# The first norm by token, and a new order of the first pairs, in a hybrid decoder trunk

## The chip, the cores and the metric

The kernel runs on 1 core of one Trainium2 chip, as one program that is launched once. The metric is device time in microseconds (us), the median of several executions. Engines are called by the profile's names: PE is TensorE (matrix products), PEld its loading of weights, DVE is VectorE, ACT is ScalarE, POOL is GpSimd, SP is SyncE, which issues nearly all DMAs here.

## The reference

One layer (`DEPTH` = 1) of a decoder trunk with 1024 features, for 1024 prompt tokens (one sequence) and 32 sample tokens (eight sequences of four) that share the weights. Cut to what matters here:

```python
mod = jax.nn.silu(c) @ w_ada[l] + b_ada[l]
sh1, sc1, gt1, sh2, sc2, gt2 = [m[:, None, :] for m in jnp.split(mod, 6, axis=-1)]
h = _rmsnorm(x, g_pre_mix[l]) * (1.0 + sc1) + sh1
z = h @ w_in[l]
...                      # gated mixing, a gated recurrence and a convolution on parts of z
y = jnp.concatenate([ya, yb, yc], axis=-1) @ w_out[l]
x = x + gt1 * _rmsnorm(y, g_post_mix[l])
h = _rmsnorm(x, g_pre_mlp[l]) * (1.0 + sc2) + sh2
y = jnp.square(jax.nn.relu(h @ w_up[l])) @ w_down[l]
x = x + gt2 * _rmsnorm(y, g_post_mlp[l])
```

`_rmsnorm` divides each token by the root of its mean square over the 1024 features. The change is in the third and fourth lines alone: the first norm, its shift and scale, and the first products with `w_in`.

## The kernel before, in words

Features lie on partitions (eight blocks k of 128), tokens along the free axis. The 1056 tokens are three chunks c of `CW` = 352; chunk 2 holds the sample tokens, whose shift and scale differ by sequence, so it is handled apart and first (`FIRST` = 2, 0, 1). Every product is made of three fast products: each operand is split into a high part (`hi`, a cast) and the rest (`lo`), and hi*hi + lo*hi + hi*lo is summed. A weight split is a cast on ACT (`whi`) and a subtraction on DVE (`wlo`).

The queues of the engines are in program order: the instructions of an engine run as the code issues them. `PE`, `ACT`, `DVE`, `POOL` and `SP` are wrappers that also keep a planner's clock by a price for each instruction; nearly all instructions therefore carry line L113 in the profile, and DMAs L107. The products of the first two weight blocks (`first_product`, L744) are issued past the wrapper. Later tasks (convolution, recurrence, norms, later shifts and gates) are generators that a planner starts at due times; none of them runs before the first products are done.

The stage in question, before:

- SP loads, in order: small vectors, x of chunks 2, 0, 1 (three parts each: `KK` = blocks 0-2, 3-5, 6-7), the identity, `ada_load(0)` (four loads of 512 KB: the weights of shift and scale for blocks 0 and 1), rows 0-1 of the first two weight blocks, `ada_load(2)`, rows 2-3. `ada_load(4)`, rows 4-7 and `ada_load(6)` follow later. `ada_load(4)` reuses the buffers of 0, and `ada_load(6)` those of 2.
- `first_squares`: ACT squares x, PE multiplies the squares with a matrix of ones and so sums them over features, with the sum of a token on every partition (`stps`, 352 columns). For chunk 1 DVE adds two blocks ahead of it. `first_rstd`: ACT takes the square root, DVE the reciprocal, of 128 x 352 values.
- `warm`: matmuls of zeros that keep PE at work.
- `ada_first(b)`: 32 matmuls for shift and scale of blocks b and b+1 (`adaps`); `ada_copy` copies the result from PSUM on ACT; `ada_turn` turns it on PE (`adapt`) and makes `mod` and `G1` on DVE.
- `first_h(p)` makes h of blocks 2p and 2p+1 for all chunks: `plain(0)`, `last()` (chunk 2), `plain(1)`, `last_lo()`, on DVE and ACT in turns. `scale_x` multiplies chunk 2 by its 1/rms on DVE ahead of that. `split_first` splits rows of the first two weight blocks, `split_next` a whole later block.
- `both(c, k)` is six products: block k, chunk c, both weight blocks.
- `first_blocks` goes over the four pairs p of blocks. In a pair: `both(0, k)`, the turn of the next pair, its h, then the weight split; `both(2, k)`, `both(1, k)`; the `ada_first` of the pair after the next; then `both` of block k+1 for chunks 0, 2, 1. `first_evacs` makes block 7 and takes the results out.

Buffers that matter: five PSUM banks in `pb`, three in `pm`; six buffers of 128 x 8 x 352 in `hp`, which hold the squares (`sqs`, three) and the h (six), so three of the h take over buffers of squares.

Of the kernel before, what the change touches and what calls it, by code (L numbers as in the profile page):

```python
# [7 lines left out]
F32 = mybir.dt.float32  # L8
F32R = mybir.dt.float32r
I32 = mybir.dt.int32  # L10
AF = mybir.ActivationFunctionType
ALU = mybir.AluOpType
# [3 lines left out]
CW = 352  # L16
# [143 lines left out]
def trunk_kernel(ctx: ExitStack, tc: tile.TileContext, xT, cT, wada0, wada, vec, cst, msk, win, wout, wup,  # L160
# [143 lines left out]
    def fetch():  # L304
        if jobs:
            src, shape = jobs.pop(0)
            raw = wp.tile(shape, F32, tag="raw", name="raw", bufs=3)
            if isinstance(src, list):
                for i, x in enumerate(src):
                    SP.dma_start(out=raw[:, 2 * i:2 * i + 2], in_=x)  # L310
            else:
                SP.dma_start(out=raw, in_=src)
            raws.append((raw, shape))
# [74 lines left out]
    def ada_load(b):  # L388

        at = []  # L390
        for k in range(0, 8, 2):
            t = ada_at[b % 4 * 2 + k // 2]
            SP.dma_start(out=t, in_=wada0[b // 2, :, k:k + 2, :])
            at += [t[:, 0, :], t[:, 1, :]]
        return b, at

    def ada_first(raws):

        b, at = raws
        ps = pb.tile([128, 128], F32, tag="b", name="adaps")  # L400
        for k in range(8):
            for g in range(4):
                PE.matmul(out=ps[32 * g:32 * g + 32, :], lhsT=scT[:, k, :], rhs=at[k][:, g * 128:g * 128 + 128],
                          start=(k == 0), stop=(k == 7), skip_group_check=True)
            if k % 2:
                yield b, ps

    def ada_copy(first):
        b, ps = first
        sb = mp.tile([128, 128], F32, tag="adasb", name="adasb")  # L410
        ACT.copy(out=sb, in_=ps)
        return b, sb

    def ada_turn(copied):

        b, sb = copied
        pt = pb.tile([128, 2, 2, 32], F32, tag="b", name="adapt")
        PE.transpose(out=pt.rearrange("p v i n -> p (v i n)"), in_=sb, identity=ident)
        add_bada(pt[:, :, :, 0:9], b, 2, 2, 8)
        DVE.scalar_tensor_tensor(out=G1[:, b:b + 2, :], in0=mod[:, 8 + b:10 + b, :],  # L420
                                 scalar=1.0, in1=bc9(V_GPM)[:, b:b + 2, :], op0=ALU.add, op1=ALU.mult)
# [187 lines left out]
    def load3(src, name):  # L609
        ts = []  # L610
        for kk, (k0, n) in enumerate(KK):
            t = e3(f"{name}{kk}")
            SP.dma_start(out=t[:, 0:n, :], in_=src[:, k0:k0 + n, :])
            ts.append(t)
        return lambda kk: ts[kk][:, 0:KK[kk][1], :]
# [26 lines left out]
    def load_rows(rows):  # L642
        for src, raw in raw_first:
            SP.dma_start(out=raw[:, rows, :], in_=src[:, rows, :])

    def split_first(rows):
        for (_, raw), (hi, lo) in zip(raw_first, w_first):
            ACT.copy(out=r(hi[:, rows, :]), in_=raw[:, rows, :])
            DVE.tensor_tensor(out=r(lo[:, rows, :]), in0=raw[:, rows, :], in1=hi[:, rows, :], op=ALU.subtract)

    xs_in = {c: load3(xT[c], f"x{c}_") for c in FIRST}
    SP.dma_start(out=ident, in_=cst[:, K_ID:K_ID + 128])
    ada_raws = [ada_load(0)]
    load_rows(slice(0, 2))
    ada_raws.append(ada_load(2))
    load_rows(slice(2, 4))

# [5 lines left out]
    def warm(n):  # L663

        for i in range(n):
            PE.matmul(out=wps[:, 0:128], lhsT=zero[:, 0:128], rhs=zero[:, 0:128], start=True, stop=True)

    sums = {}

    def first_squares(c, kk, added):  # L670

        k0, n = KK[kk]
        sq = sqs[c]
        if kk == 0:
            sums[c] = pb.tile([128, CW], F32, tag="b", name="stps")
        ACT.activation(out=sq[:, k0:k0 + n, :], in_=xs_in[c](kk), func=AF.Square)
        if added:
            DVE.tensor_tensor(out=sq[:, k0, :], in0=sq[:, k0, :], in1=sq[:, k0 + 1, :], op=ALU.add)
        for k in range(k0, k0 + n):
            if not added or k != k0 + 1:  # L680
                PE.matmul(out=sums[c], lhsT=ones, rhs=sq[:, k, :], start=k == 0, stop=k == (6 if added else 7))

    def first_rstd(c):
        ACT.activation(out=rstds[c], in_=sums.pop(c), func=AF.Sqrt, scale=1.0 / 1024, bias=eps)
        DVE.reciprocal(out=rstds[c], in_=rstds[c])

    def spans(p):

# [5 lines left out]
    def scale_x(c, p):  # L694
        for kk, a, b, k in spans(p):
            t = xs_in[c](kk)[:, a:b, :]
            DVE.tensor_tensor(out=t, in0=t, in1=rep(rstds[c], b - a), op=ALU.mult)

    def first_h(p):


        if p == 0:
            h.update({c: (hc(f"h{c}hi"), hc(f"h{c}lo")) for c in range(NCH)})

        def plain(c):
            ts = [(xs_in[c](kk)[:, a + i, :], k + i) for kk, a, b, k in spans(p) for i in range(b - a)]
            for t, k in ts:
                DVE.scalar_tensor_tensor(out=t, in0=t, scalar=G1[:, k, 0:1], in1=rstds[c], op0=ALU.mult,
                                         op1=ALU.mult)
                ACT.activation(out=r(h[c][0][:, k, :]), in_=t, func=AF.Identity, bias=sh1[:, k, 0:1], scale=1.0)  # L710
            for t, k in ts:
                DVE.scalar_tensor_tensor(out=r(h[c][1][:, k, :]), in0=t, scalar=sh1[:, k, 0:1],
                                         in1=h[c][0][:, k, :], op0=ALU.add, op1=ALU.subtract)

        def last():
            w = CW - NS
            for kk, a, b, k in spans(p):
                n = b - a
                u = xs_in[2](kk)[:, a:b, :]
                us_ = u[:, :, w:]  # L720
                DVE.tensor_tensor(out=b4(us_), in0=b4(us_), in1=seqs(G1[:, k:k + n, :]), op=ALU.mult)
                DVE.tensor_tensor(out=b4(us_), in0=b4(us_), in1=seqs(sh1[:, k:k + n, :]), op=ALU.add)
                for i in range(n):
                    ACT.activation(out=u[:, i, 0:w], in_=u[:, i, 0:w], func=AF.Identity, scale=G1[:, k + i, 0:1],
                                   bias=sh1[:, k + i, 0:1])
                ACT.copy(out=r(h[2][0][:, k:k + n, :]), in_=u)

        def last_lo():
            for kk, a, b, k in spans(p):
                hi, lo = (t[:, k:k + b - a, :] for t in h[2])  # L730
                DVE.tensor_tensor(out=r(lo), in0=xs_in[2](kk)[:, a:b, :], in1=hi, op=ALU.subtract)

        plain(0)
        last()
        plain(1)
        last_lo()

    pss = {}

# [7 lines left out]
    def both(c, k):  # L747
        for m, i in ((0, 0), (0, 1), (1, 0), (1, 1), (0, 2), (1, 2)):
            first_product(c, k, m, i)

    warm(14)
    for i, c in enumerate(FIRST):
        for kk in range(3):
            first_squares(c, kk, i == 2)
            if i == 1 and kk == 0:
                first_rstd(2)
                scale_x(2, 0)
        if i == 0:
            nc.scalar.preload_act_table(AF.Sqrt)
    first_rstd(0)  # L760
    parts = ada_first(ada_raws.pop(0))
    for i in range(3):
        next(parts)
        warm(2)
    first_rstd(1)
    nc.scalar.preload_act_table(AF.Sigmoid)
    split_first(slice(0, 2))
    copied = ada_copy(next(parts))
    ada_raws.append(ada_load(4))
    load_rows(slice(4, 8))  # L770
    warm(2)
    ada_turn(copied)
    first_h(0)
    scale_x(2, 1)
    for at in ada_first(ada_raws.pop(0)):
        warm(2)
    copied = [ada_copy(at)]
    ada_raws.append(ada_load(6))
    fetch()
    SP.dma_start(out=cst_t[:, K_BLK:K_BLK + 256], in_=cst[:, K_BLK:K_BLK + 256])  # L780

    def first_blocks():


        for p in range(4):
            k = 2 * p
            both(0, k)
            if p < 3:
                ada_turn(copied.pop())
                first_h(p + 1)  # L790
                if p < 2:
                    scale_x(2, p + 2)
                    split_first(slice(2 * p + 2, (4, 8)[p]))
                else:
                    split_next()
            else:
                ACT.copy(out=r(means), in_=cst_t[:, K_BLK:K_BLK + 256])
            both(2, k)
            both(1, k)
            if p < 2:  # L800
                for at in ada_first(ada_raws.pop(0)):
                    pass
                copied.append(ada_copy(at))
            if p < 3:
                for c in (0, 2, 1):
                    both(c, k + 1)

    def first_evacs(evacs):
        credit.update(dve=0.0, act=0.0, pe=0.0)
# [1286 lines left out]
```

## Time and profile before

| | us |
|---|---|
| median of 3 runs | 1260.38 |
| the three runs | 1264.3, 1258.51, 1260.38 |
| the profiled execution | 1263.86 |
| its span in the profile | 1262.1 |
| granted clock of PE, mean | 0.99 |

| engine | busy, us | share of the span |
|---|---|---|
| PE | 1221.9 | 97% |
| PEld | 1171.4 | 93% |
| DVE | 902.0 | 71% |
| ACT | 533.6 | 42% |
| POOL | 63.0 | 5% |

How to read the views: a row of the timeline has start, length, engine, line, operation, output<-inputs, shapes and count, and in brackets how long the engine was idle before it and what ended that. A row of the busy time by stretches has the stretch, its length, the busy time of PE, PEld, DVE, ACT and POOL with the number of instructions, the granted clock, the share of the DMA engines' time and GB/s. All times are from the start of the span. The ends of matmuls are modelled, so the distance from start to start tells more than a length. A float32 matmul shows as two passes.

### The profile page before, as it was taken

To read this page: it belongs to the slowest core of one execution; us is meant where nothing else is said; L and a number is where in the kernel's file an instruction comes from. 1 tells how busy PE (TensorE), PEld (TensorE's weight loads), DVE (VectorE), ACT (ScalarE), POOL (GpSimd) and SP (SyncE) were. 2 spreads that over 40 slices of the span, in tenths; PEclk is the share of its full clock that TensorE was granted. 3 is DMA by queue.
4 is the path that set the end of the run, shared out by engine and by line. 5 is a ranking of instruction groups with operands and counts; after the bars stand their busy time and mean duration, and the time that the engine had idled before them with its cause. 6 is when DMAs were issued, how large, how long until landed. Compare 5 with 4: busy or idle time off the path is not lost.

```text
span 1262.1 us, 20853 instructions
## 1 busy us (share of the span) xinstructions
PE 1221.9 (97%) x8614; PEld 1171.4 (93%) x8614; DVE 902.0 (71%) x1469; ACT 533.6 (42%) x989; POOL 63.0 (5%) x107
## 2 busy tenths in 40 slices
PE   9999999999899999999999999999999999999995
PEld 7888889999889999899999999999999999999994
DVE  5799889688658768866686657657666765765766
ACT  6513464684854746555423312322331331231533
POOL 1000020211010011000000000000000000000001
PEclk9999999999999999999999999999999999999998
DMA  9458401111111466243201211210211120111218
GB/s 367 170 217 277 168 26 52 43 59 47 35 43 40 151 192 182 85 134 106 79 18 50 68 34 34 68 49 19 68 50 34 51 68 32 36 67 35 108 18 210
DMA packets 48846, 113.22 MB, mean 90 GB/s; under 512 B 10336, under 2 KB 24832, under 8 KB 48624
## 3 DMA queue, kind: packets, MB, share of 16 engines
q1 hardware_dynamic: 44432, 99.22, 22.9%
q0 software_dynamic: 4320, 12.68, 4.3%
q8 instruction: 67, 1.10, 0.4%
q14 instruction: 27, 0.22, 0.1%
HBM read 101.75 MB, written 10.14 MB: 89 GB/s over the span
## 4 chain that ended last, share of the span: by engine, by line
PE 78%; DVE 11%; ACT 6%; DMA 3%; issue 2%; POOL 0%; SPq 0%; DVEq 0%; ACTq 0%
PE pmt L113 71%; DVE acc L113 2%; PE adaps L113 1%; DMA rawada<-in_wada 1%; DVE T L113 1%; PE pmt L744 1%; DVE wlo L113 1%; DMA o<-in_xT 1%; ACT K L113 1%; ACT vf L113 1%; DVE q L113 1%; PE sc L113 1%; DVE rsq L113 1%; ACT relu L113 1%; PE ob L113 1%
## 5 line engine op out<-in xcount | busy, mean ns | idle before, releaser
L113 PE MATMUL pmt<-ah,whi 128*128 128x352 f32 (+2 forms) x744 | 244.0, 328 | 7.9 <-DVE acc L113 5.8
L113 PE MATMUL pmt<-al,whi 128*128 128x352 f32 (+2 forms) x744 | 241.3, 324 | 1.3 <-DVE al L113 1.3
L113 PE MATMUL pmt<-ah,wlo 128*128 128x352 f32 (+2 forms) x744 | 240.1, 323 | 0.0
L113 DVE TENSOR_TENSOR acc<-acc,pmt 128x352 f32<-128x352 f32 (+1 forms) x320 | 158.5, 510 | 91.8 <-PE pmt L113 91.6
L113 DVE TENSOR_TENSOR wlo<-raw,whi 128x1024 fp32r<-128x1024 f32 (+2 forms) x113 | 134.5, 1192 | 46.2 <-ACT whi L113 46.2
L113 ACT CAST whi<-raw 128x1024 fp32r<-128x1024 f32 (+2 forms) x113 | 114.2, 1014 | 107.9 <-PE pmt L113 105.8
L113 PEld LDWEIGHTS pmt<-ah,whi 128*128 128x128 f32 x744 | 139.7, 188 | 15.3 <-DVE acc L113 10.7
L113 PEld LDWEIGHTS pmt<-al,whi 128*128 128x128 f32 x744 | 139.9, 188 | 4.2 <-DVE al L113 2.0
L113 PEld LDWEIGHTS pmt<-ah,wlo 128*128 128x128 f32 x744 | 139.9, 188 | 0.4
L113 ACT COPY acc<-pmt 128x352 f32<-128x352 f32 x63 | 28.4, 452 | 196.7 <-PE pmt L113 161.8
L113 PE MATMUL pmt<-h22hi,wlo 128*128 128x352 f32 x256 | 82.7, 323 | 0.0
L113 PE MATMUL pmt<-h22hi,whi 128*128 128x352 f32 x256 | 82.5, 322 | 0.0
L113 PE MATMUL pmt<-h22lo,whi 128*128 128x352 f32 x256 | 82.3, 322 | 0.0
L113 DVE SCALAR_TENSOR_TENSOR cva<-cvx,vec_t,cva 128x1024 f32<-128x1024 f32 x60 | 77.7, 1295 | 1.2
L113 PE MATMUL pmt<-s,whi 128*128 128x352 f32 x312 | 75.6, 324 | 0.0
L113 ACT ACTIVATE relu<-pmt 128x352 f32<-128x352 f32 x57 | 26.4, 463 | 104.2 <-PE pmt L113 101.3
L113 DVE TENSOR_TENSOR al<-rsq,ah 128x352 fp32r<-128x352 f32 x96 | 49.1, 523 | 15.7 <-ACT ah L113 9.6
L113 PE MATMUL pmt<-h1hi,whi 128*128 128x352 f32 x168 | 55.7, 332 | 2.6 <-DVE gq L113 2.6
L113 PE MATMUL pmt<-h2hi,whi 128*128 128x352 f32 x168 | 56.7, 337 | 0.0
L113 PE MATMUL pmt<-h0hi,whi 128*128 128x352 f32 x168 | 55.5, 330 | 0.8 <-DVE gq L113 0.8
L113 PEld LDWEIGHTS pmt<-s,whi 128*128 128x128 f32 x312 | 54.5, 188 | 0.0
L113 DVE TENSOR_TENSOR rsq<-relu 128x352 f32<-128x352 f32 x45 | 23.5, 523 | 43.0 <-ACT relu L113 41.8
(391 smaller groups left out, 2941.0 us busy)
## 6 DMA issues: line engine op xcount, KB each, us to landing
rawada<-in_wada SPq DMA_DIRECT2D x48, 512.0 KB, 8.3
raw<-in_wup SPq DMA_DIRECT2D x36, 512.0 KB, 3.5
raw<-in_wdn SPq DMA_DIRECT2D x48, 256.0 KB, 3.1
raw<-in_win SPq DMA_DIRECT2D x22, 512.0 KB, 3.6
raw<-in_wout SPq DMA_DIRECT2D x20, 512.0 KB, 3.5
raw<-in_wdn SPq DMA_DIRECT2D x12, 512.0 KB, 3.5
x<-in_xT SPq DMA_DIRECT2D x6, 528.0 KB, 7.0
o<-in_xT POOLq DMA_DIRECT2D x6, 528.0 KB, 7.8
```

The lines of the kernel that those rows point to most:

```text
L113: return f(**kw)
L744: nc.tensor.matmul(out=pss[m, c], lhsT=r(w_first[m][i % 2][:, k, :]), rhs=r(h[c][i // 2][:, k, :]), start=k == i == 0, stop=k == 7 and i == 2)
```

## The change

Four parts:

1. The sums of the first norm are made by token. For each block, four matmuls take 88 tokens of the squares each as weights and one column of ones, and add into a tile of 88 x 4 sums, which a matmul with zeros has cleared first. ACT takes the square root of 88 x 4 values (`token_rms`, which exists for the last norm), DVE the reciprocal; `first_diagonal` multiplies it into four copies of the 88 x 88 identity, in a part of the squares' buffer; `by_feature` (exists too) spreads it over all partitions with a matmul with the ones, and ACT copies the result to `rstds`. The additions on DVE for chunk 1 go.
2. The identity is loaded ahead of x. x of chunk 1 is loaded behind the first shift and scale and the first weight rows, and it is squared and summed behind the first turn, between the first products. The Sqrt table is loaded before all squares, the Sigmoid table behind the last square root.
3. `first_h` returns its parts, so that the first pair can be issued in the order `plain(0)`, split, `both(0, 0)`, `last`, `last_lo`, `both(2, 0)`, `plain(1)`, with the squares of chunk 1 in between.
4. In the pairs, `both(0, k)` and `both(2, k)` come first, then `ada_first` of the next pair, `both(1, k)`, the turn, the weight split, and only then the next pair's h. `ada_first(2)`, `ada_load(6)`, the next weight load and the load of the constants move into the first pair.

```diff
-    xs_in = {c: load3(xT[c], f"x{c}_") for c in FIRST}
     SP.dma_start(out=ident, in_=cst[:, K_ID:K_ID + 128])
+    xs_in = {c: load3(xT[c], f"x{c}_") for c in FIRST[0:2]}
     ada_raws = [ada_load(0)]
     load_rows(slice(0, 2))
+    xs_in[1] = load3(xT[1], "x1_")
     ada_raws.append(ada_load(2))
     load_rows(slice(2, 4))
...
-    def first_squares(c, kk, added):
+    def first_squares(c, kk):
         k0, n = KK[kk]
         sq = sqs[c]
         if kk == 0:
-            sums[c] = pb.tile([128, CW], F32, tag="b", name="stps")
+            sums[c] = pb.tile([CW // 4, 4], F32, tag="b", name="sums")
+            PE.matmul(out=sums[c], lhsT=zero[:, 0:CW // 4], rhs=zero[:, 0:4], start=True, stop=False,
+                      skip_group_check=True)
         ACT.activation(out=sq[:, k0:k0 + n, :], in_=xs_in[c](kk), func=AF.Square)
-        if added:
-            DVE.tensor_tensor(out=sq[:, k0, :], in0=sq[:, k0, :], in1=sq[:, k0 + 1, :], op=ALU.add)
+        t = CW // 4
         for k in range(k0, k0 + n):
-            if not added or k != k0 + 1:
-                PE.matmul(out=sums[c], lhsT=ones, rhs=sq[:, k, :], start=k == 0, stop=k == (6 if added else 7))
-
-    def first_rstd(c):
-        ACT.activation(out=rstds[c], in_=sums.pop(c), func=AF.Sqrt, scale=1.0 / 1024, bias=eps)
-        DVE.reciprocal(out=rstds[c], in_=rstds[c])
+            for g in range(4):
+                PE.matmul(out=sums[c][:, g:g + 1], lhsT=sq[:, k, g * t:(g + 1) * t], rhs=ones[:, 0:1],
+                          start=False, stop=k == 7, skip_group_check=True)
+
+    def first_rms(c):
+        rts[c] = token_rms(sums.pop(c))
+
+    def first_diagonal(c):
+        t = CW // 4
+        rt = rts.pop(c)
+        DVE.reciprocal(out=rt, in_=rt)
+        d = sqs[c][0:t, 0, :]
+        DVE.tensor_tensor(out=d.rearrange("p (g t) -> p g t", t=t), in0=rep(ident[0:t, 0:t], 4),
+                          in1=rt.rearrange("p (g o) -> p g o", o=1).to_broadcast([t, 4, t]), op=ALU.mult)
+        return d
+
+    def first_rstd(c, d):
+        ACT.copy(out=rstds[c], in_=by_feature(d))
...
+    nc.scalar.preload_act_table(AF.Sqrt)
     warm(14)
-    for i, c in enumerate(FIRST):
-        for kk in range(3):
-            first_squares(c, kk, i == 2)
-            if i == 1 and kk == 0:
-                first_rstd(2)
-                scale_x(2, 0)
-        if i == 0:
-            nc.scalar.preload_act_table(AF.Sqrt)
-    first_rstd(0)
+    for kk in range(3):
+        first_squares(2, kk)
+    first_squares(0, 0)
+    first_rms(2)
+    d = first_diagonal(2)
+    first_squares(0, 1)
+    first_rstd(2, d)
+    first_squares(0, 2)
+    scale_x(2, 0)
+    first_rms(0)
+    d = first_diagonal(0)
+    warm(2)
+    first_rstd(0, d)
     parts = ada_first(ada_raws.pop(0))
     for i in range(3):
         next(parts)
         warm(2)
-    first_rstd(1)
-    nc.scalar.preload_act_table(AF.Sigmoid)
-    split_first(slice(0, 2))
-    copied = ada_copy(next(parts))
+    copied = [ada_copy(next(parts))]
     ada_raws.append(ada_load(4))
     load_rows(slice(4, 8))
     warm(2)
-    ada_turn(copied)
-    first_h(0)
-    scale_x(2, 1)
-    for at in ada_first(ada_raws.pop(0)):
-        warm(2)
-    copied = [ada_copy(at)]
-    ada_raws.append(ada_load(6))
-    fetch()
-    SP.dma_start(out=cst_t[:, K_BLK:K_BLK + 256], in_=cst[:, K_BLK:K_BLK + 256])
...
     def first_blocks():
+        ada_turn(copied.pop())
+        first_squares(1, 0)
+        plain, last, last_lo = first_h(0)
+        plain(0)
+        split_first(slice(0, 2))
+        both(0, 0)
+        first_squares(1, 1)
+        last()
+        first_squares(1, 2)
+        first_rms(1)
+        nc.scalar.preload_act_table(AF.Sigmoid)
+        last_lo()
+        d = first_diagonal(1)
+        both(2, 0)
+        first_rstd(1, d)
+        plain(1)
+        scale_x(2, 1)
         for p in range(4):
             k = 2 * p
-            both(0, k)
+            if p:
+                both(0, k)
+                both(2, k)
+            if p < 3:
+                for at in ada_first(ada_raws.pop(0)):
+                    if p == 0:
+                        warm(2)
+                copied.append(ada_copy(at))
+                if p == 0:
+                    ada_raws.append(ada_load(6))
+                    fetch()
+                    SP.dma_start(out=cst_t[:, K_BLK:K_BLK + 256], in_=cst[:, K_BLK:K_BLK + 256])
+            both(1, k)
             if p < 3:
                 ada_turn(copied.pop())
-                first_h(p + 1)
                 if p < 2:
-                    scale_x(2, p + 2)
                     split_first(slice(2 * p + 2, (4, 8)[p]))
                 else:
                     split_next()
+                plain, last, last_lo = first_h(p + 1)
+                plain(0)
+                last()
+                plain(1)
+                last_lo()
+                if p < 2:
+                    scale_x(2, p + 2)
+                for c in (0, 2, 1):
+                    both(c, k + 1)
             else:
                 ACT.copy(out=r(means), in_=cst_t[:, K_BLK:K_BLK + 256])
-            both(2, k)
-            both(1, k)
-            if p < 2:
-                for at in ada_first(ada_raws.pop(0)):
-                    pass
-                copied.append(ada_copy(at))
-            if p < 3:
-                for c in (0, 2, 1):
-                    both(c, k + 1)
```

More of the change, by code (lines that the diff above doesn't have):

```diff
@@ L666, in warm @@
             PE.matmul(out=wps[:, 0:128], lhsT=zero[:, 0:128], rhs=zero[:, 0:128], start=True, stop=True)
-    sums = {}
-    def first_squares(c, kk, added):
+    sums, rts = {}, {}
+    def first_squares(c, kk):
         k0, n = KK[kk]
@@ L731, in last_lo @@
                 DVE.tensor_tensor(out=r(lo), in0=xs_in[2](kk)[:, a:b, :], in1=hi, op=ALU.subtract)
[L733 to L736, printed above, removed]
+        return plain, last, last_lo
     pss = {}
```

## The prediction

> **What bounds the kernel now.** I read the busy time by stretches, the timeline of the first 63 us engine by engine, what TensorE (PE) waited for there, and the chain of waits. The change touches only what runs before the product of the third weight block, which begins at 62.95, so the question is how far that moment moves.
>
> ```profile
> 62.97:200.00 137.03, 136.41 (x1104) 120.83 (x1104) 125.82 (x150) 51.67 (x95) 10.79 (x20) 1.00 0.49 167
> 7.44:29.87 22.43, 22.43 (x203) 14.98 (x204) 13.85 (x20) 15.81 (x23) 0.00 (x0) 1.00 1.03 405
> 29.87:62.95 33.08, 30.68 (x278) 28.06 (x277) 25.59 (x56) 17.93 (x36) 0.25 (x2) 0.95 0.52 181
> 62.95 0.33 PE L113 MATMUL pmt<-h0hi,whome 128*128 128x352 f32 x1
> ```
>
> The first three lines give length, then busy time of PE, weight load, DVE, ACT, POOL, then granted clock, DMA share and GB/s. Behind the stage PE is busy 136.4 of 137.0 us and DVE 125.8, so neither has slack to swallow a delay: a us lost or won before 62.95 is a us of the end. From 7.44 to 29.87 PE has no gap at all: its own order of work sets the start of the products, although the DMA engines are full too (share 1.03). From 29.87 on it has 2.4 us of gaps and a clock of 0.95.
>
> ```profile
> 7.44 12.84 PE L113 MATMUL stps<-sq,cst_t 128*128 128x352 f32 x42
> 20.21 0.64 PE L113 MATMUL adaps<-rawada,scT 128*32 128x128 f32 x16
> 24.98 0.27 PE L113 MATMUL adapt<-cst_t,adasb 128*128 128x128 f32 x1
> 29.87 0.41 PE L744 MATMUL pmt<-h0hi,whi 128*128 128x352 f32 x1
> 30.92 0.27 PE L113 MATMUL adapt<-cst_t,adasb 128*128 128x128 f32 x1
> 33.29 1.96 PE L113 MATMUL adaps<-rawada,scT 128*32 128x128 f32 x64
> 36.23 0.32 PE L744 MATMUL pmt<-h2hi,whi 128*128 128x352 f32 x1
> 37.18 0.32 PE L744 MATMUL pmt<-h1hi,whi 128*128 128x352 f32 x1
> 40.94 0.43 PE L744 MATMUL pmt<-h0hi,wlo 128*128 128x352 f32 x1 [1.92 <-DVE wlo L113]
> 42.32 0.41 PE L113 MATMUL adapt<-cst_t,adasb 128*128 128x128 f32 x1
> 51.88 0.27 PE L113 MATMUL adapt<-cst_t,adasb 128*128 128x128 f32 x1
> 18.25 7.48 DMA rawada<-in_wada
> ```
>
> These are the timeline's PE rows (start, length, operation, count, wait) and one step of the chain of waits, which releases the first h. 21 matmuls with the ones (two passes each, 42) take 12.84 us, 0.61 each. The first shift/scale block takes 24.98 - 20.21 = 4.8 us with its warm matmuls, a later one 1.96. Six products of one block and chunk ("a sextet") take 37.18 - 36.23 = 0.95. The turns (adapt) stand at 24.98, 30.92, 42.32, 51.88: each releases mod and G and so the next h, and each follows the first sextet of its pair. The row at 40.94 is the stall that the weight splits cause by standing behind h on DVE.
>
> **The price of a sum by token.** The same sums by token are in the trace near its end:
>
> ```profile
> L113 PEld LDWEIGHTS sums<-cst_t,tots x16: 133/156/178, 1236.6 to 1247.9; 128*112 128x112 f32 x8, 128*64 128x64 f32 x8
> 1236.59 0.88 PEld L113 LDWEIGHTS sums<-cst_t,tots 128*112 128x112 f32 x8
> 1247.52 0.54 PEld L113 LDWEIGHTS sums<-cst_t,tots 128*64 128x64 f32 x8 [1.71 <-DVE tots L113]
> 1238.09 0.24 ACT L113 ACTIVATE rt<-sums,cst_t 112x4 f32<-112x4 f32 x1
> 1238.36 0.18 DVE L113 RECIPROCAL rt<-rt 112x4 f32<-112x4 f32 x1 [0.70 <-ACT rt L113]
> L113 DVE TENSOR_TENSOR diag<-cst_t,rt x2: 417/522/628, 1238.6 to 1248.7; 112x448 f32<-112x448 f32 x1, 64x256 f32<-64x256 f32 x1
> L113 ACT COPY acc<-pmt 128x352 f32<-128x352 f32 x63 | 28.4, 452 | 196.7 <-PE pmt L113 161.8
> ```
>
> Eight passes of 112 tokens step by (0.88 - 0.18)/7 = 0.100 us, of 64 tokens by (0.54 - 0.13)/7 = 0.058. The change has 88 tokens: halfway, 0.079. A feature block is four matmuls of two passes, 0.63 us against 0.61 before, and a chunk 5.05. So PE gains nothing by the new form; the third chunk, where DVE adds halved part of the matmuls (5 instead of 8, 3.1 us), loses 2.0. Each chunk also gets a zero matmul (two passes with 88 columns as weights, 0.16) and the spreading matmul (like one with the ones, 0.6). PE's work in the stage grows by 2 x 0.2 + 2.0 + 3 x 0.76 = 4.7 us, and two warm matmuls that stand in a wait. The unknown end: at 0.058 a chunk costs 3.7, at 0.100 6.4; three chunks give -4.0 to +4.0 us on PE, and since some of it fills stalls I keep about -3 to +3. The gain, on engines that do not set the end there:
>
> ```profile
> 13.10 2.35 DVE L113 RECIPROCAL rstd<-rstd 128x352 f32<-128x352 f32 x1 [7.79 <-ACT rstd L113]
> 16.30 1.60 DVE L113 TENSOR_TENSOR sq<-sq 128x352 f32<-128x352 f32 x3
> 10.58 1.08 ACT L113 ACTIVATE sq<-x 128x1056 f32<-128x1056 f32 x1
> 9.29 1.28 ACT L759 ACT_TABLE_LOAD   x1
> ```
>
> Three reciprocals (2.35 each) become 0.18 + about 0.52 for the diagonal, and the three additions go; DVE had 8.6 us idle in 7.44 to 29.87. The Sqrt table load moves ahead of the first x and is hidden there. The Sigmoid load moves behind the third square root, where its follower waits for PE's spreading matmul anyway.
>
> **Order on the queues.** Taking x's third chunk (1.4 MB at 405 GB/s, 3.5 us) out of the way lets the first shift/scale land 3.5 us sooner, about 17.1 instead of 12.0 + 8.6 = 20.6 (row below: the last of four is issued at about 12.0). The identity goes ahead of x and costs the first square 0.2. The third chunk now comes behind all of x, four loads of 512 KB and the first weight rows, some 7 MB: 17.3 us at 405 GB/s after a start near 3, an estimate of 21; it is first squared at 26.2, so the move costs nothing.
>
> ```profile
> 8.37 3.93 SPq L107 DMA_DIRECT2D rawada<-in_wada  x4
> rawada<-in_wada SPq DMA_DIRECT2D x16, 512.0 KB, 8.6
> ```
>
> The last shift/scale load waits for buffers of the second, which PE now frees only between about 36.8 and 41; behind it on SP's queue stand a weight load and the small constants. They land by 41 + 8.6 = 50, and are wanted at 61 and later. POOL issues nothing else. So no DMA ends on the path, by a cover of ten us.
>
> **The new lead-in, step by step (us).** First square ends 7.5; PE sums chunk 2 to 12.6 and blocks 0 to 5 of chunk 0 to 16.5, then spreads chunk 2's 1/rms (0.6). On ACT the copy of that result (0.45) stands ahead of the last square of chunk 0 (0.78), so PE waits from 17.1 to 18.55 (1.4). Blocks 6 and 7 to 19.8, two warm matmuls; square root, reciprocal and diagonal (0.24 + 0.2 + 0.52 with hand-overs) end at 21.1: a wait of 0.85. Spread to 21.7, shift/scale 4.6 us, first turn at 26.3, against 24.98: 1.3 later in spite of the earlier data. Now PE sums chunk 1 in between: it waits for the square that ACT starts only after the copy for the turn (0.76), 3 blocks, the first sextet (0.4 wait for the weight split), 5 blocks (0.55 wait), a sextet, the diagonal (0.35 wait), spread: 36.2. The second shift/scale with warm matmuls 4.8, a sextet, second turn at 42.0. Before it stood at 30.92. Of those 11 us, 1.9 are two sextets that used to come after it.
>
> **The cycle of the other pairs.** Before, a turn needed only the first sextet of its pair, and its shift/scale was done a pair earlier. Now turn p+1 stands behind both sextets 0 and 2, then shift/scale p+1, then sextet 1; and the second part of h2 is the last thing that DVE makes. So the work no longer overlaps:
>
> ```profile
> 42.78 0.20 DVE L113 TENSOR_TENSOR mod<-adapt,vec_t 128x36 f32<-128x36 f32 x1 [1.55 <-PE adapt L113]
> 48.35 0.89 DVE L113 TENSOR_TENSOR h2lo<-x,h2hi 128x704 fp32r<-128x704 f32 x1
> 40.47 0.76 DVE L113 TENSOR_TENSOR wlo<-raw,whi 128x256 fp32r<-128x256 f32 x2
> 49.95 1.29 DVE L113 TENSOR_TENSOR wlo<-raw,whi 128x512 fp32r<-128x512 f32 x2
> 58.57 1.22 DVE L113 TENSOR_TENSOR whome<-raw,whome 128x1024 fp32r<-128x1024 f32 x1
> ```
>
> Turn to mod 0.46, mod to the end of h2lo 49.24 - 42.78 = 6.46, and the weight split's DVE part, now ahead of h: 0.76, 1.29 and 1.22 (its casts on ACT run while PE still does the third sextet). From h2lo to the next turn PE needs 0.3 + 1.96 + 0.95 = 3.2. Cycles: 0.46 + 6.46 + 0.76 + 3.2 = 10.9, then 11.4. Turns at 42.0, 52.9, 64.3. The last h2lo at 64.3 + 8.1 = 72.4; then 0.3 + 0.95 + 18 products of 0.16 = 4.1. The stage ends at 76.5 instead of 62.95: +13.5. It counts what the change saves: the stalls for the split (1.92 and smaller) and the slow clock behind them are inside 62.95.
>
> **The clock.** In each cycle PE does four sextets (3.8 us) while it waits 6.5 to 8 us for h: about 3.3 us idle inside 4.2.
>
> ```profile
> 37.89:41.30 3.41, 1.19 (x6) 0.62 (x5) 3.33 (x7) 1.12 (x4) 0.12 (x1) 1.00 0.45 171
> 41.30:44.71 3.41, 3.41 (x14) 3.34 (x13) 1.70 (x5) 0.87 (x2) 0.00 (x0) 0.50 0.02 5
> 328.02:331.43 3.41, 1.75 (x11) 1.75 (x12) 3.41 (x7) 3.33 (x8) 0.00 (x0) 1.00 0.00 0
> 331.43:334.84 3.41, 2.95 (x48) 2.62 (x48) 3.31 (x5) 3.32 (x8) 0.00 (x0) 1.00 0.36 113
> 525.99:529.40 3.41, 1.50 (x9) 1.47 (x10) 2.57 (x4) 1.62 (x4) 0.00 (x0) 1.00 0.15 60
> 529.40:532.82 3.42, 3.42 (x14) 3.42 (x13) 3.35 (x7) 0.97 (x3) 0.00 (x0) 0.50 0.02 5
> ```
>
> Stretches of 3.41 us with PE busy 1.19 or 1.50 us are followed by one at half clock, one with 1.75 is not. Where the stretches will lie I cannot know; an idle of 1.9 us inside one is enough, and 3.3 in 4.2 gives it in most positions. I take two half-clock stretches in three cycles, 1.5 us each where PE is what the chain waits for: +3.0, between 0 and 5. The Trainium skill ("TensorE: Matmul & The Clock Gate", "Why this matters for your kernels") warns only of PE-idle gaps above about 3 us. By that rule no gap here (the longest 2.5) slows the clock and the sum would be 13.5; but the stretch from 37.89 has no gap of 3 us and is followed by half clock, so the trace speaks against it.
>
> **Sum.** 13.5 + 3.0 = +16.5. The profiled execution took 1263.86 (span 1262.1) and would take 1280.4; the median of the three runs is 3.5 lower, so 1276.9, said as 1277. With the cheap sum and no half clock 1260.4 + 10.5 = 1270.9; with the dear one and three such stretches 1260.4 + 13.5 + 3 + 5 = 1281.9. Later tasks are placed by a planner that counts the prices of these instructions; I cost that at nothing, since its clocks meet at the last turn in both kernels, but allow 2 us either way.
>
> **Rivals.** (1) No half clock, because each 3.41 us stretch happens to hold less than 1.7 us of idle or the pauses are cut up by the sextet between them: 1260.4 + 13.5 = 1273.9; against it the rows above. 20%. (2) Not slower: the stage is led by DMA, as the chain has it, whose step of 7.48 us on the shift/scale loads ends at 25.73 with the first x times G. Then the 3.5 us earlier landing moves the whole stage: 1256.9. It decides if the first turn comes before 21.5 and no later turn falls behind; against it PE's 22.43 busy us of 22.43. 4%. (3) Only the lead-in is lost (about 8 us net of the two sextets) and the three cycles stay at their old 9.6: 1268 to 1269. It needs the second part of h2 early, against the 6.46. 9%. (4) h1 and h2 take over the buffers of the squares, and their first writes wait for chunk 1's diagonal and spread more than I have; if the first h1 then misses the cover of the second shift/scale, that costs up to its 4.8: 1282. 7%.
>
> **Numbers.** The forecast, one to three half-clock stretches, has 60%. The range 1267 to 1283 leaves out rival 2 and the far end of 4. About 0.5% (6.3 us) is what this measurement tells from no change: slower 93%, same 5% (half of rival 2, the lowest end of 3), faster 2%.
>
> **What would show it.** Right: turns near 26, 42, 53 and 64, waits of PE on h2lo and h2hi of 1 to 2.5 us in each pair, one to three half-clock stretches before 77, the third weight block's first product near 76 to 80. Sums by token right: 64 passes of a chunk in about 5 us. Wrong: a first turn before 23, a turn-to-turn time below 10, or the same shift not found at the end because later waits gave it back.

## The result and the profile after

The changed kernel takes 1296.6 us, the median of 4 runs (1294.69 to 1297.14), against 1260.58 for the kernel before: a ratio of 1.028, 95% interval 1.0253 to 1.0306. It is slower, as forecast, but by 36 us instead of 16, and lies above the range. Its profiled execution took 1294.69, with a span of 1292.9 and a mean granted clock of 0.976 (before: 0.99).

All of the loss is in the stage ahead of the third weight block's product. That product starts at 94.29 instead of 62.95, 31.3 us later; from there to the end of the span are 1198.6 us, against 1199.15 before. (In the ten traces of this document that last part runs from 1194.2 to 1200.2 us, so 0.5 us there says nothing.) The other 4.7 us between 31.3 and the 36.0 of the medians come from the two profiled executions: that of before lay 3.3 us above its median, that of after 1.9 below, less these 0.5. So stage differences against the profile before read some 3 us short of the times.

The timeline of the kernel after, PE's groups of rows (start, length, operation, shapes, count, wait ahead of it):

```profile
7.41 7.71 PE L113 MATMUL sums<-cst_t,sq 128*88 128x1 f32 x64 [0.53 <-ACT sq L113]
15.28 7.18 PE L113 MATMUL sums<-cst_t,sq 128*88 128x1 f32 x48
...
25.07 2.50 PE L113 MATMUL sums<-cst_t,sq 128*88 128x1 f32 x16 [1.23 <-ACT sq L113]
...
36.40 0.27 PE L113 MATMUL adapt<-cst_t,adasb 128*128 128x128 f32 x1
37.29 2.04 PE L113 MATMUL sums<-cst_t,sq 128*88 128x1 f32 x24 [0.53 <-ACT sq L113]
...
41.34 5.92 PE L113 MATMUL sums<-cst_t,sq 128*88 128x1 f32 x40
...
56.49 0.27 PE L113 MATMUL adapt<-cst_t,adasb 128*128 128x128 f32 x1
69.19 0.27 PE L113 MATMUL adapt<-cst_t,adasb 128*128 128x128 f32 x1
82.19 0.27 PE L113 MATMUL adapt<-cst_t,adasb 128*128 128x128 f32 x1
94.29 0.32 PE L113 MATMUL pmt<-h0hi,whome 128*128 128x352 f32 x1
```

Read the sums first. Compare 24 passes in 2.04 us at 37.29 with 40 passes in 5.92 at 41.34 (0.148 each) and 48 in 7.18 at 15.28 (0.150): the same instruction has two prices. Then read the four turns: the first comes at 36.40, where 26.3 was forecast. What parts the two prices is in the busy time by stretches of the same kernel (length, then busy time of PE, weight load, DVE, ACT, POOL, then granted clock, DMA share, GB/s):

```profile
7.41:36.40 28.99, 27.63 (x219) 23.63 (x220) 2.29 (x5) 6.35 (x11) 0.00 (x0) 0.59 0.79 302
9.49:12.90 3.41, 3.41 (x26) 3.41 (x26) 0.00 (x0) 1.25 (x2) 0.00 (x0) 0.50 1.03 418
12.90:16.31 3.41, 3.41 (x26) 3.41 (x25) 0.70 (x2) 1.08 (x2) 0.00 (x0) 0.50 1.02 403
16.31:19.73 3.42, 3.42 (x25) 3.42 (x25) 0.00 (x0) 0.15 (x1) 0.00 (x0) 0.50 1.05 397
...
33.38:36.79 3.41, 3.37 (x51) 2.61 (x47) 0.09 (x1) 0.81 (x2) 0.00 (x0) 1.00 0.76 259
36.40:56.49 20.09, 19.17 (x170) 16.44 (x169) 8.19 (x19) 10.02 (x18) 0.00 (x0) 0.75 0.44 147
56.49:69.00 12.51, 9.81 (x101) 8.47 (x100) 7.45 (x19) 4.86 (x11) 0.25 (x2) 0.86 0.32 119
69.00:82.00 13.00, 10.33 (x103) 8.99 (x102) 7.69 (x16) 5.27 (x11) 0.00 (x0) 0.87 0.43 111
82.00:94.29 12.29, 9.62 (x59) 8.85 (x58) 7.51 (x16) 6.82 (x13) 0.00 (x0) 1.00 0.56 213
```

From 9.49 to 33.38 the granted clock is 0.50 throughout. In the three stretches from 9.49 to 19.73 there is no gap: PE and its weight load are busy for the whole 3.41 us. Nothing waits there, PE has work all the time, and it still runs at half clock. The Trainium skill ("TensorE: Matmul & The Clock Gate", "What's actually happening") says that the clock follows how busy PE has been of late. The rows above fit that only if a busy row of the profile is not what is counted. A second half-clock span, 40.20 to 50.45, lies over the third chunk's sums; two single stretches, at 64.1 and 77.8, lie in the cycles of the pairs.

### The profile page after: what moved, and what is told of

It reads as the page before. It is cut to its first block, busy times and chain, and to the rows that moved or that the text cites. A ratio compares the mean times of both kernels' runs of the same rounds, so it can differ in the third digit from the quotient of the medians.

```text
span 1292.9 us, 21189 instructions
## 1 busy us (share of the span) xinstructions
PE 1243.2 (96%) x8780; PEld 1193.1 (92%) x8780; DVE 901.3 (70%) x1469; ACT 532.2 (41%) x991; POOL 69.2 (5%) x107
## 4 chain that ended last, share of the span: by engine, by line
PE 62%; DVE 7%; ACT 4%; issue 2%; DMA 1%; POOL 0%; DVEq 0%; ACTq 0%; POOLq 0%
PE pmt L113 60%; DVE acc L113 2%; DVE T L113 1%; DMA o<-in_xT 1%; DVE wlo L113 1%; DVE rsq L113 1%; ACT relu L113 1%; PE sc L113 0%; PE stps L113 0%; DVE o L113 0%; ACT K L113 0%; DVE al L113 0%; ACT vf L113 0%; DVE rstd L113 0%; ACT h21hi L113 0%
## 5 line engine op out<-in xcount | busy, mean ns | idle before, releaser
L113 PE MATMUL pmt<-h2hi,wlo 128*128 128x352 f32 x168 | 54.6, 325 | 0.0
L113 PE MATMUL pmt<-h2lo,whi 128*128 128x352 f32 x168 | 54.6, 325 | 0.0
```

The source lines that it names most:

```text
L113: return f(**kw)
```

## The experiments

A column of the moving operand "streams" when it passes through PE against the loaded weights. Two theories stood against each other. **S** (the expectations call it G): matmuls with one column stream next to nothing, so the clock drops, however busy the rows look; the sums by token cost far more than the forecast has. **W**: the new order makes PE wait, and its waits bring the half clock. A third, **L**, says that such passes are slow by themselves (88 columns of weights each). The rest of the loss is then the order of the pairs (**P**).

**Ones again, new order.** The sums go back to matmuls with the ones, with all else as after:

```diff
-            for g in range(4):
-                PE.matmul(out=sums[c][:, g:g + 1], lhsT=sq[:, k, g * t:(g + 1) * t], rhs=ones[:, 0:1],
-                          start=False, stop=k == 7, skip_group_check=True)
+            PE.matmul(out=sums[c], lhsT=ones, rhs=sq[:, k, :], start=k == 0, stop=k == 7)
...
     def first_rms(c):
-        rts[c] = token_rms(sums.pop(c))
+        ACT.activation(out=rstds[c], in_=sums.pop(c), func=AF.Sqrt, scale=1.0 / 1024, bias=eps)
...
     def first_diagonal(c):
...
+        DVE.reciprocal(out=rstds[c], in_=rstds[c])
```

> The changed order with the old sums: matmuls of the ones with 352 columns of squares (eight for each chunk, no additions on DVE), square root and reciprocal of 128 x 352. Theory G (the clock is granted by the columns that stream through PE, and a one-column matmul counts as idle): full clock from 7 us to at least 40; turns near 22, 37, 49, 60; the third weight block starts near 74 (73 to 76); about 1277 us. Rival W (the half clock comes from PE's new waits for ACT's squares and copies, which stay in this kernel): half clock in much of 9 to 30 again, first turn after 28, third weight block after 86, about 1289 us.

Measured: 1273.74 (ratio to before 1.0102, 1.0087 to 1.0117). Its windows and its timeline:

```profile
7.44:57.70 50.26, 43.11 (x367) 31.85 (x371) 30.43 (x56) 25.52 (x44) 0.25 (x2) 1.00 0.80 291
```

```profile
22.89 0.27 PE L113 MATMUL adapt<-cst_t,adasb 128*128 128x128 f32 x1
...
74.58 0.32 PE L113 MATMUL pmt<-h0hi,whome 128*128 128x352 f32 x1
```

The order is that of after and PE waits 7.2 of the 50.3 us, yet the clock is full; only one stretch, at 57.8, is at half. W falls for the long half-clock spans. The stage ends 19.7 us sooner than after's: so much the sums by token cost. The first turn comes at 22.89, 2.1 us ahead of before's. That is what the moved third chunk takes out of PE's way and not more: 32 passes with the ones (9.88 us) now stand ahead of it instead of 42 (12.84). The earlier shift/scale data let it happen; that they gain anything beyond this isn't shown.

**The same passes, 96 equal columns.** Each sum is made 96 times side by side, with the same weights, the same number of passes and the same order:

```diff
-            sums[c] = pb.tile([CW // 4, 4], F32, tag="b", name="sums")
+            sums[c] = pb.tile([CW // 4, 4, 96], F32, tag="b", name="sums")
...
-                PE.matmul(out=sums[c][:, g:g + 1], lhsT=sq[...], rhs=ones[:, 0:1], ...)
+                PE.matmul(out=sums[c][:, g, :], lhsT=sq[...], rhs=ones[:, 0:96], ...)
...
-        rts[c] = token_rms(sums.pop(c))
+        rts[c] = token_rms(sums.pop(c)[:, :, 0])
```

> The changed kernel with 96 columns of ones instead of one as the moving operand of each sum by token (one of the 96 equal results is used); the clearing matmul has 384 columns. G: full clock through the sums, a pass steps by 0.085 to 0.10 us instead of 0.12 to 0.15; first turn near 28 instead of 36.4; third weight block near 82 instead of 94.3; about 1284 us, faster than the changed kernel by 12 although PE does 96 times the work. W, and rival L (these passes are slow by themselves): no faster, 1297 to 1302.

Measured: 1281.77 (1.0173, 1.0156 to 1.019): 96 times the columns, and 15 us less than after. Its windows (a stretch of the sums, then the two that lead into its first half clock) and its timeline:

```profile
7.84:11.25 3.41, 3.41 (x45) 3.41 (x44) 0.00 (x0) 2.65 (x3) 0.00 (x0) 1.00 1.03 416
...
48.80:52.21 3.41, 1.21 (x6) 0.85 (x6) 2.56 (x7) 1.89 (x4) 0.12 (x1) 1.00 0.04 16
52.21:55.62 3.41, 3.41 (x62) 2.96 (x64) 0.82 (x2) 0.00 (x0) 0.12 (x1) 0.50 0.02 5
```

```profile
7.46 5.51 PE L113 MATMUL sums<-cst_t,sq 128*88 128x96 f32 x64 [0.80 <-ACT sq L113]
13.46 4.12 PE L113 MATMUL sums<-cst_t,sq 128*88 128x96 f32 x48
27.73 0.27 PE L113 MATMUL adapt<-cst_t,adasb 128*128 128x128 f32 x1
81.91 0.33 PE L113 MATMUL pmt<-h0hi,whome 128*128 128x352 f32 x1
```

PE and weight load are busy 3.41 of 3.41, just as in after, but at clock 1.00, and 64 passes take 5.51 (0.086 each). L falls: the passes are not slow by themselves. S holds in this: with more columns in the same passes the clock stays full. Half clock comes only at 52.2 and 76.1, each behind a stretch with PE idle for most of it (1.21 and 0.91 us busy of 3.41).

**How many columns.** The same edit with 32 and with 64 in the place of 96; one run each.

> As the run with 96 columns, with 32. At full clock 32 columns of a float32 pass stream for 32 x 0.84 ns = 0.027 us of a step of 0.082, a third. G with a bound at 35 to 50% of a 3.41 us stretch: still half clock through the sums, first turn near 36, third weight block near 93 to 95. If any column beyond the first were enough: full clock, first turn near 27, third weight block near 81.

> As the run with 96 columns, with 64: streaming 0.054 of 0.082 us, two thirds. G with a bound at 35 to 50%: full clock, first turn near 27, third weight block near 81.

Windows of the kernel with 32 columns, and then windows and timeline of that with 64, for the first two stretches of sums:

```profile
8.10:11.51 3.41, 3.41 (x46) 3.41 (x46) 0.00 (x0) 2.58 (x3) 0.00 (x0) 1.00 1.02 416
11.51:14.92 3.41, 3.41 (x26) 3.41 (x24) 0.70 (x2) 1.23 (x2) 0.00 (x0) 0.50 1.05 419
```

```profile
7.35:10.76 3.41, 2.96 (x38) 2.96 (x38) 0.00 (x0) 2.75 (x4) 0.00 (x0) 1.00 1.03 418
10.76:14.18 3.42, 3.42 (x43) 3.30 (x42) 0.66 (x2) 1.54 (x3) 0.00 (x0) 1.00 1.03 415
```

```profile
13.32 3.90 PE L113 MATMUL sums<-cst_t,sq 128*88 128x64 f32 x48
...
27.31 0.27 PE L113 MATMUL adapt<-cst_t,adasb 128*128 128x128 f32 x1
...
81.41 0.33 PE L113 MATMUL pmt<-h0hi,whome 128*128 128x352 f32 x1
```

With 32 columns a full stretch of sums is followed by half clock, and the kernel takes 1292.77, with the third block at 92.91; with 64 the clock stays, and it takes 1282.73, with the third block at 81.41. An estimate of the share: a matmul with the ones streams 2 x 352 columns in 0.61 us, 0.87 ns each; so a pass of about 0.08 us streams for 0.028 us with 32 columns, a third, and for 0.055 with 64, two thirds. The bound lies between. That does not clash with the stretches of idle PE in the prediction, where 1.50 busy of 3.41 us (44%) was followed by half clock and 1.75 (51%) was not; but a busy row is not streaming time, as these kernels show, so the two shares are not the same measure.

The pair after and 64 columns has the same order and the same passes and differs in the clock: 94.29 - 81.41 = 12.9 us of the sums' 19.7 are half clock. The other 6.8 (81.41 - 74.58) part the 64-column kernel from the one with the ones. Of these, 5.6 lie ahead of the second turn (43.63 against 38.04), the work and the waits that the new form adds; 1.2 lie in the cycles of the pairs, where the 64-column kernel has two half-clock stretches and the one with the ones has one.

**Sums by token alone, old order.** The before kernel with the new sums, the identity ahead of x and the table loads moved; x's third chunk, the pairs and the splits as before:

```diff
+    for kk in range(3):
+        first_squares(2, kk)
+    first_squares(0, 0)
+    first_rms(2)
+    d = first_diagonal(2)
+    first_squares(0, 1)
+    first_squares(0, 2)
+    first_rstd(2, d)
+    scale_x(2, 0)
+    first_squares(1, 0)
...
```

> The kernel before with the sums and 1/rms by token alone: all of x is loaded and summed ahead of the first shift and scale, pairs in the old order; no wait of PE for ACT between the sums of a chunk. G: half clock from about 9.5 us to the end of the sums near 40, first turn near 46, third weight block near 85 (83 to 87), about 1282 us. W: full clock, first turn near 34, third weight block near 71, about 1269 us.

Measured: 1286.97 (1.0212, 1.0196 to 1.0227). Its window over the sums, and the first turn and the third block from its timeline:

```profile
8.10:42.20 34.10, 32.73 (x221) 30.45 (x224) 2.98 (x7) 7.94 (x13) 0.00 (x0) 0.50 0.56 219
```

```profile
47.86 0.33 PE L113 MATMUL adapt<-cst_t,adasb 128*128 128x128 f32 x1 [1.51 <-ACT adasb L113]
85.49 0.33 PE L113 MATMUL pmt<-h0hi,whome 128*128 128x352 f32 x1
```

Without the new order the half clock is longer still, 34 us in one piece, as all three chunks are summed in a row: the sums bring it, not the order. The stage ends 22.5 us behind that of before (85.49 against 62.95).

**Old pairs, new sums.** After, with the loop over the pairs as before (second shift/scale ahead of the loop; both(0, k), turn, split, h, both(2, k), both(1, k), next shift/scale):

```diff
             if p:
                 both(0, k)
-                both(2, k)
-            if p < 3:
-                for at in ada_first(ada_raws.pop(0)):
...
-            both(1, k)
             if p < 3:
                 ada_turn(copied.pop())
...
+            if p:
+                both(2, k)
+            both(1, k)
+            if p < 2:
+                for at in ada_first(ada_raws.pop(0)):
+                    pass
+                copied.append(ada_copy(at))
```

> The changed kernel with the turn of the next pair behind the first sextet again and shift/scale a pair ahead (weight split still ahead of h). The cycle theory (a turn that waits for the second part of h2, shift/scale and a sextet makes a cycle of 11 to 13 us): first turn still near 36, second near 55, then distances of 7 to 9 us instead of 12.7 and 13.0; third weight block near 85 instead of 94.3; about 1287 us. Rival (the cycle is set by DVE's h alone, so the place of the turn costs nothing): distances stay above 11, 1296 us.

Measured: 1286.86 (1.0209, 1.0194 to 1.0224). Its timeline:

```profile
56.64 0.27 PE L113 MATMUL adapt<-cst_t,adasb 128*128 128x128 f32 x1
63.82 0.27 PE L113 MATMUL adapt<-cst_t,adasb 128*128 128x128 f32 x1
71.76 0.32 PE L113 MATMUL adapt<-cst_t,adasb 128*128 128x128 f32 x1
85.63 0.32 PE L113 MATMUL pmt<-h0hi,whome 128*128 128x352 f32 x1
```

Up to the second turn it is after, us for us (56.64 and 56.49). Then the turns step by 7.2 and 7.9 instead of 12.7 and 13.0, and the stage ends 8.7 us sooner. P is shown: a turn that stands behind both(2, k) and the next shift/scale lengthens the cycle. The two half-clock stretches in after's cycles are gone as well (granted clock 1.00 from 56.64 to 85.63), so the 8.7 us hold both.

**Both undone.** Ones for the sums and the old pairs; what stays of the change is x's third chunk behind the first turn, the identity ahead of x, the moved table loads, the first pair's new order, and the split ahead of h.

> The changed order of loads and of the first pair, with the old sums and the turns in their old place: what is left is the third chunk's loading, squares and sums behind the first turn (and the weight split ahead of h). From the row durations: turns near 22, 37, 44, 53, third weight block near 66 against 62.95 of before: the second turn still waits for the third chunk's sums; about 1264 us. Rival (the earlier data pays once the sums keep the clock): third weight block before 62, 1259 us or less.

Measured: 1264.71 over 10 runs (1.0033, 1.0023 to 1.0042). Its timeline, three of the turns and the third block:

```profile
22.44 0.27 PE L113 MATMUL adapt<-cst_t,adasb 128*128 128x128 f32 x1
36.24 0.27 PE L113 MATMUL adapt<-cst_t,adasb 128*128 128x128 f32 x1
...
51.48 0.33 PE L113 MATMUL adapt<-cst_t,adasb 128*128 128x128 f32 x1
65.35 0.32 PE L113 MATMUL pmt<-h0hi,whome 128*128 128x352 f32 x1
```

Taken off one after the other, the parts of the 31.3 us are: sums 19.7 (94.29 - 74.58), pairs 9.2 (74.58 - 65.35), the rest of the order 2.4 (65.35 - 62.95). In the medians the same steps are 22.9, 9.0 and 3.9. In another order they come out a little otherwise: the pairs 8.7 with the new sums, the sums 22.5 in the old order. The moved third chunk loses a little: the first turn gains 2.5 us (22.44), and the second gives more than that back (36.24 against 30.92), since the third chunk is now squared and summed between the first products. The 2.4 us hold the split ahead of h as well, which gains by itself (next run).

**The split alone.** The before kernel, with only the weight split set ahead of the next pair's h:

```diff
+                if p < 2:
+                    split_first(slice(2 * p + 2, (4, 8)[p]))
                 first_h(p + 1)
                 if p < 2:
                     scale_x(2, p + 2)
-                    split_first(slice(2 * p + 2, (4, 8)[p]))
```

> The kernel before, with the weight splits of rows 2-3 and 4-7 ahead of the next pair's h and nothing else. PE's stall of 1.9 us for the low part of the weights goes, and with it mostly the half-clock stretch behind it; h comes 0.8 and 1.3 us later, which PE covers by two sextets and shift/scale. Third weight block near 60 instead of 62.95, about 1258 us, 0.2% faster. Rival (h is what the stage waits for, so the split ahead of it costs what it saves): no change.

Measured: 1255.82 over 6 runs against 1260.79 over 17: ratio 0.9963 (0.995 to 0.9977). It beats both kernels. Its window of the pairs, its timeline, and what PE waited for up to 60 us (total, times, longest):

```profile
24.00:59.44 35.44, 33.95 (x361) 30.47 (x361) 29.11 (x66) 21.69 (x43) 0.25 (x2) 1.00 0.66 231
```

```profile
30.36 0.27 PE L113 MATMUL adapt<-cst_t,adasb 128*128 128x128 f32 x1
38.52 0.27 PE L113 MATMUL adapt<-cst_t,adasb 128*128 128x128 f32 x1
46.74 0.33 PE L113 MATMUL adapt<-cst_t,adasb 128*128 128x128 f32 x1
59.44 0.33 PE L113 MATMUL pmt<-h0hi,whome 128*128 128x352 f32 x1
```

```profile
PE pmt L744 <- DVE h2lo L113: 1.5, 2, 1.2
PE stps L113 <- ACT sq L113: 0.7, 1, 0.7
```

The wait for wlo (1.92 us at 40.94 before) is gone, and with it the half-clock stretch from 41.30 that followed it. The third turn comes 3.8 us sooner than before (42.32), the third block 3.5. The edit acts behind the second turn, which is 0.6 us early already; from there to the third turn are 8.2 us instead of 11.4. This one edit of the change pays, in the old pair order; alone in the new one it was not tried. The medians differ by 5.0 us, more than the stage. The rest lies behind it, 1194.2 us instead of 1199.15, with one half-clock stretch instead of three up to 600 us; that the edit brings this isn't shown.

## Why the prediction was wrong

**The step that failed** is "The price of a sum by token" together with "The clock". The price, 0.079 us a pass, was right at full clock: the 24 passes in the 2.04 us from 37.29, read as the prediction read its rows (less the 0.22 of the last one), step by 0.079, and the groups of 64 and 96 columns took 0.081 (48 in 3.90) and 0.086 a pass with their ends. But its rows came from a place with 8 such passes at a time, where the clock was still full, and the prediction carried it to 64 in a row. There the pass cost 0.15 once the clock was at half, and the first 64 took 7.71 us instead of about 5. The term for half clock was sized, at 3.0 with a range of 0 to 5, from stretches where PE was idle; the sums themselves, with PE busy all the time, had no half clock in it. Measured, that term is about 16: 12.9 over the sums, and some 3 in the cycles.

Interval by interval, the forecast (without half clock), after, and the kernel with 64 columns, whose sums run at full clock:

| | forecast | after | 64 columns |
|---|---|---|---|
| first turn | 26.3 | 36.40 | 27.31 |
| to the second | 15.7 | 20.09 | 16.32 |
| to the third | 10.9 | 12.70 | 12.78 |
| to the fourth | 11.4 | 13.00 | 11.37 |
| to the third weight block | 12.2 | 12.10 | 13.63 |
| sum | 76.5 | 94.29 | 81.41 |

- **The lead-in** missed by 10.1 and 4.4 us, and all but 1.6 of these 14.5 are gone in the column on the right: the clock, not the steps. PE's added work, the copy ahead of the last square and the sextets that moved were sized well.
- **The cycles** hold. In after, the third and fourth intervals are 1.8 and 1.6 over the sum, and each has one half-clock stretch (64.1 and 77.8): the two stretches of 1.5 us that the prediction added. That there are two is in part luck: the same order with the ones had one (57.8). With 64 columns the stretches fall at 51.7 and 75.6, and it is the third and the last interval that are 1.9 and 1.4 over, while the fourth, without one, is 11.37 against 11.4.
- **The cause of the longer cycle** holds as well. What PE waited for in after, up to 95 us:

```profile
PE pmt L755 <- DVE h2lo L113: 3.7, 2, 2.2
PE pmt L755 <- ACT h2hi L113: 2.8, 3, 1.2
PE sums L113 <- ACT sq L113: 2.3, 3, 1.2
PE pmt L755 <- DMA cvhist<-in_sconv: 1.5, 1, 1.5
PE pmt L755 <- DVE wlo L113: 0.2, 1, 0.2
```

  The waits for the second part of h2 are of the size that was named (1 to 2.5 each); of those for wlo 0.2 us is left. The wait that is put down to a DMA (cvhist, a small load for the convolution) is one for h2lo, too: it ends at 77.09, when h2lo is ready, the weight load of the same product has h2lo as its releaser, and with 32 columns the list has three waits for h2lo and no DMA.
- **The saving on DVE and ACT** was read rightly as worth nothing in time: from 7.41 to 36.40 DVE was busy 2.29 us, and the first turn came later.
- **Behind the stage** nothing is given back that stands out from the spread of the traces: 1198.6 against 1199.15.

Of the 19.6 us between forecast and time, 14.8 lie in the stage (94.29 against 76.5 + 3.0). The other 4.8 are in how the profiled executions stand to their medians (the prediction took 3.5 off for that of before, and that of after lay 1.9 on the other side), less the 0.5 behind the stage.

**The rivals.** No half clock at all (1) is the opposite of what came. The lead by DMA (2) fell; where the sums are made with the ones the first turn does come 2.1 to 2.5 us sooner, but PE then has 10 passes less ahead of it. Only the lead-in lost (3) fell: the third and fourth intervals are 12.7 and 13.0 instead of 9.6, and the old pairs gave 8.7 us back. In (4), buffers of h1 and h2, no wait of the size needed shows up. None of the four had the mechanism that decided, and a fifth should have stood there: half clock from the sums themselves.

What the runs do not settle is what the hardware counts. Columns streamed explain 1, 32, 64 and 96 columns, with a bound at a share of a pass between a third and two thirds; the work done in the array or what it writes would fit these runs as well.

## What to carry to other kernels

Before you rewrite a reduction into matmuls with few columns, look at the columns that stream, not only at the busy time: in these runs a chain of one-column matmuls filled PE's row and still left its clock at half, for itself and for what came right behind it. A price read from a few such instructions at full clock need not hold for many. When the order of a pipelined loop is changed, look for what releases the next turn and count what now stands ahead of it; and try the parts of a change one by one, since here one small edit of the change, tried alone, paid (0.9963) while the whole lost 2.8%.

## What the runs showed of the hardware that was not expected

- Half clock with no idle: PE and weight load busy 3.41 of 3.41 us at a granted clock of 0.50, in three stretches on end. The half clock lasted 23.9 us in all (34 us with three chunks in a row), with little idle in it.
- A wider matmul can be faster: 64 passes took 7.71 us with 1 column and 5.51 with 96, and the whole kernel 1296.6 and 1281.77.
- The bound lies between 32 columns (half clock) and 64 (full clock), for passes of about 0.08 us with 88 columns of weights.
- Weight loads slow down along with the clock: in the kernel before, a load of 128 columns took 0.19 us at 41.05 and 0.33 at 42.83, where the clock was half. The step of a pass with one column and 88 columns of weights went from 0.085 us (the group at 37.29, with its ends) to 0.148 (that at 41.34).
- In the pairs, half clock still follows a stretch with little PE work (1.21 of 3.41 us with 96 columns), and removing one wait of 1.92 us removed one such stretch: the wait and the stretch together were 3.2 us between two turns (11.4 to 8.2).
